# Seven-product down projection: the low part of the second weight sums is issued behind the additions of the second product group

## The chip, the cores and the metric

The kernel runs on one core of a Trainium2 chip. A core has TensorE (matrix products; PE in the profile, its weight loads PEld), VectorE (DVE), ScalarE (ACT), GpSimd (POOL) and SyncE (SP, which issues most transfers here). Each engine works through its own list of instructions in order, and the engines wait for one another by semaphores. The metric is the device time of one execution in microseconds (us), as the median of several runs.

## The reference

The reference is a decoder trunk of two layers on 512 tokens of width 1024. Each layer is a half-step SwiGLU feed-forward, a mixer (gated linear attention in layer 0, stick-breaking attention in layer 1) and a second half-step feed-forward, all in float32:

```python
def swiglu(h, w_gate, w_up, w_down):
    return (jax.nn.silu(h @ w_gate) * (h @ w_up)) @ w_down

for i in range(DEPTH):                       # DEPTH = 2, D_MODEL = 1024, D_FF = 2816, SEQ = 512
    x = x + 0.5 * swiglu(rmsnorm(x, ffn1_norm[i]), ffn1_w_gate[i], ffn1_w_up[i], ffn1_w_down[i])
    x = x + mixer(rmsnorm(x, mix_norm[i]))
    x = x + 0.5 * swiglu(rmsnorm(x, ffn2_norm[i]), ffn2_w_gate[i], ffn2_w_up[i], ffn2_w_down[i])
return rmsnorm(x, final_norm)
```

The change concerns the product with `w_down` in the four feed-forwards.

## The kernel before

**Numbers in two parts.** Each float32 operand is split into a high part (`wh`, `hh`, `nh`: a conversion on ScalarE, line 143 for weights, 852 for activations) and a low part (`wl`, `hl`, `nl`: the operand minus its high part, a subtraction on VectorE, lines 144 and 853). Each product is then three matmuls: high by high, low weight by high, high weight by low.

**Tiling.** The 512 tokens are the moving side and the rows of the weights are the contraction. The 2816 columns of the hidden layer are worked in six groups (`GROUPS`); the hidden columns of one group are multiplied by their rows of `w_down` and added to the residual tiles `xs` while the next groups' gate and up products run. For the groups 1 and 3 (`DOWN_SEVEN`), 512 hidden columns each, the down product is done by `seven_down`: the 2x2 blocks of weights and activations are combined so that seven block products do the work of eight. It is called twice for a group (`part` 0 and 1, each for 256 lower and 256 upper outputs), so four times in a feed-forward and sixteen times in the kernel.

**One call of `seven_down`** puts two entries on the feed, `body_1` and `body_2`. TensorE works in three PSUM tiles for each of two column blocks `m`: `w` (`ws`, lines 414 to 416), `z` (`zs`) and `q` (`qs`, both `m` in one bank). `prod` (line 396, its matmuls at line 401) issues six matmuls of 256 moving columns.

- `body_1`: a11 by b11 into `w`; ScalarE copies `w` to `z` (line 420); the first sums by t1 into `q` and two additions of `q` to x; then by t2 into `w`, each followed by an addition of `w` to x; then a2 by b21 into `z`, each followed by an addition of `z`.
- `body_2`: the second sums by t3 into `w`, copied to `u3` by ScalarE (line 448) and added to x; by b22 into `q`, added; a2 by t4 into `w`, added.

All additions go through `add` (line 405), whose instruction on VectorE stands at line 407. The sums of weight blocks are made on VectorE: the first at lines 385 and 386, the second at 392 and 393.

**How weights get split.** `Feed.start` (line 147) looks ahead: it splits the entries that come up, and for the entry after `body_1` of a seven it leaves the split out (the test of `e.second` and of `copied`). So the second sums of a call are split by `body_1` itself, at line 421: `v["second"].split(v["copied"])`. There the high part on ScalarE carries an order edge, `tc.issue_after(after)`, to the copy of `w` into `z`; the low part on VectorE has none. The second sums themselves, and the transfers behind them, were made at the start of `body_1`.

**What sets the order.** Nothing in this part of the kernel is pinned by hand. A planner orders each engine's instructions when the program is built: an instruction's place in the program is its priority, `ahead()` raises it, and of the instructions whose inputs are ready by the planner's own estimate of time the one with the highest priority goes first. `tc.issue_after(i)` adds, for what its block puts on the engine of `i`, the condition that it is placed behind `i`; it adds no semaphore. On the chip the order is then fixed, and an engine waits at an instruction whose semaphores have not come.

Of the kernel before, what the change touches and what calls it, by code (L numbers as in the profile page):

```python
# [10 lines left out]
F32 = mybir.dt.float32  # L11
# [4 lines left out]
ALU = mybir.AluOpType  # L16
# [14 lines left out]
def turns(t):  # L31

    return t.rearrange("p (two n) -> p n two", two=2)


def flat(ps):

    return ps.rearrange("p (n two) -> p two n", two=2)


def pair(t):

    return t.rearrange("p (two n) -> p two n", two=2)
# [3 lines left out]
def decoder(ctx: ExitStack, tc: tile.TileContext, a: dict, out: bass.AP):  # L47
    nc = tc.nc
# [12 lines left out]
    def psum(name, tag=None):  # L61
        if tag is None:
            tag = order[turn_[0] % 8]
            turn_[0] += 1
        return pp.tile([P, T], F32, tag=tag, bufs=banks[tag], name=name)
# [42 lines left out]
    class Entry:  # L108
# [11 lines left out]
                self.views = [view(ch.load()) for ch, view, _, _ in self.units]  # L120
            return self.views

        def split(self, after=None):
            if self.W is None:
                self.W = []
                for r, (_, _, n, m) in zip(self.view(), self.units):
                    self.W.append(self.parts(r, n, m, after))

        def parts(self, r, n, m, after):
            few = n * m < 1024  # L130
            if few:

                h, l = (
                    st["few"].tile([P, n * m], F32R, tag="v" + t, bufs=1, name="w" + t) for t in "hl"
                )
            else:
                h, l = (wp.tile([P, n * m], F32R, tag="w" + t, bufs=4, name="w" + t) for t in "hl")
            h, l = (t.rearrange("p (n m) -> p n m", m=m) for t in (h, l))
            pieces = r if isinstance(r, tuple) else (r,)
            for i, part in enumerate(pieces):  # L140
                k = slice(i * n // len(pieces), (i + 1) * n // len(pieces))
                with tc.issue_after(after) if after is not None else ExitStack():
                    nc.scalar.copy(h[:, k], part)  # L143
                nc.vector.tensor_tensor(out=l[:, k], in0=part, in1=h[:, k].bitcast(F32), op=ALU.subtract)  # L144
            return h, l

    class Feed:
# [51 lines left out]
    def ahead():  # L199

        return tc.high_priority(4000)
# [163 lines left out]
    def seven_down(pool, w, r0, hs, part):  # L365

        H = T // 2
        lower, upper = (  # L370
            Chunk(w[r0 : r0 + 4 * P, c : c + 256].rearrange("(f p) c -> p f c", p=P), 4, 256)
            for c in (part * 256, 512 + part * 256)
        )
        lower.few = upper.few = True
        v = {}

        def halves():

            lo, up = (c.load().rearrange("p (c two) d -> p two c d", two=2) for c in (lower, upper))
            return lo[:, 0], lo[:, 1], up[:, 0], up[:, 1]  # L380

        def sums_12(_):
            a11, _, a21, a22 = halves()
            s = v["s12"] = pool().tile([P, 4, 256], F32, tag="s", bufs=4, name="s12")
            nc.vector.tensor_tensor(out=s[:, 0:2], in0=a21, in1=a22, op=ALU.add)
            nc.vector.tensor_tensor(out=s[:, 2:4], in0=s[:, 0:2], in1=a11, op=ALU.subtract)
            return s

        def sums_34(_):
            a11, a12, a21, _ = halves()  # L390
            s = pool().tile([P, 4, 256], F32, tag="s", bufs=4, name="s34")
            nc.vector.tensor_tensor(out=s[:, 0:2], in0=a11, in1=a21, op=ALU.subtract)
            nc.vector.tensor_tensor(out=s[:, 2:4], in0=a12, in1=v["s12"][:, 2:4], op=ALU.subtract)
            return s

        def prod(ps, w, k0, m, b, first):
            for c in range(2):
                bh, bl = (turns(t) for t in hs[c][b])
                wh, wl = (t[:, k0 + c, m * P : (m + 1) * P] for t in w)
                for n, (l_, r_) in enumerate(((wh, bh), (wl, bh), (wh, bl))):  # L400
                    st["pe"] = nc.tensor.matmul(  # L401
                        ps, l_, r_, start=first and c + n == 0, stop=c == 1 and n == 2, skip_group_check=True
                    ).ins

        def add(m, up, col, ps):
            x = pair(xs[part * 2 + m + 4 * up][:, col * H : col * H + H])
            nc.vector.scalar_tensor_tensor(out=x, in0=ps, scalar=0.5, in1=x, op0=ALU.mult, op1=ALU.add)

        def body_1(W):
            a11, s, v["a2"] = W  # L410
            ws, zs, qs = [], [], []
            for m in range(2):
                ws.append(psum("ps_w")[:, 0:H])
                prod(ws[m], a11, 0, m, "b11", True)
            for m in range(2):


                zs.append(psum("ps_z")[:, 0:H])
                with ahead():
                    v["copied"] = nc.scalar.copy(zs[m], ws[m]).ins  # L420
            v["second"].split(v["copied"])
            yield

            ps = psum("ps_q")
            for m in range(2):
                qs.append(ps[:, m * H : (m + 1) * H])
                prod(qs[m], s, 0, m, "t1", m == 0)
            for m in range(2):
                add(m, 1, 1, flat(qs[m]))
            yield  # L430
            for m in range(2):
                prod(ws[m], s, 2, m, "t2", False)
                add(m, 0, 1, flat(ws[m]))
            yield
            for m in range(2):
                prod(zs[m], v["a2"], 0, m, "b21", False)
                add(m, 0, 0, flat(zs[m]))
            v["w"], v["q"] = ws, qs
            yield

        def body_2(W):
            (s,) = W
            ws, qs = v["w"], v["q"]

            u3 = pool().tile([P, 2, H], F32, tag="c", bufs=1, name="u3")
            for m in range(2):
                prod(ws[m], s, 0, m, "t3", False)
                nc.scalar.copy(pair(u3[:, m]), flat(ws[m]))
                add(m, 1, 1, pair(u3[:, m]))
            yield  # L450
            for m in range(2):
                prod(qs[m], s, 2, m, "b22", False)
            for m in range(2):
                add(m, 0, 1, flat(qs[m]))
            yield
            for m in range(2):
                prod(ws[m], v["a2"], 2, m, "t4", False)
                add(m, 1, 0, flat(ws[m]))
            yield

        units = [(lower, lambda t: halves()[0], 2, 256), (lower, sums_12, 4, 256), (lower, lambda t: halves()[1::2], 4, 256)]
        feed.q.append(Entry(units, body_1))
        feed.q.append(Entry([(lower, sums_34, 4, 256)], body_2))
        v["second"] = feed.q[-1]
        feed.q[-1].second, feed.q[-1].v = True, v
# [896 lines left out]
    class SB:  # L1362
# [28 lines left out]
        def evac_q(self, p, ps):  # L1391
            t = self.qp.tile([P, T], F32, tag="n", bufs=2, name="n")
            nc.vector.scalar_tensor_tensor(
                out=pair(t), in0=flat(ps), scalar=0.125, in1=pair(st["R"]), op0=ALU.mult, op1=ALU.mult
            )

            def parts(cast):
                for e in range(2):
                    own, oth = slice(e * 64, e * 64 + 64), slice(64 - e * 64, 128 - e * 64)
                    m = self.qp.tile([P, T], F32R, tag="mq", name="mq")  # L1400
                    cast(m[own], t[own])
                    nc.vector.tensor_tensor(out=m[oth], in0=t[own], in1=m[own].bitcast(F32), op=ALU.subtract)
                    self.qk[p, e, "q"] = m

            self.later.append(parts)
            if not self.hold:
                self.parts()
# [543 lines left out]
```

## Time and profile before

| | |
|---|---|
| median of 3 runs | 1775.71 us (1775.12 to 1776.97) |
| the profiled execution | 1776.0 us, span of its instructions 1774.1 us |
| granted TensorE clock in it | 0.999 |
| busy share of ScalarE, GpSimd | 61%, 3% |
| conversions to high parts of sums (line 143) | 176, 1053 ns each |
| additions of line 407 | 64 from `q`, 64 from `w`, 32 from `z`, 32 from `u3`; about 418 ns each |

The difference between the profiled execution and its span, 1.9 us, lies before the first and behind the last instruction. In the rows of a timeline the columns are the start and the duration in us, engine, line, operation, tile written and tiles read, shape and count; brackets hold the idle time of that engine just before and what is held to have ended it. Consecutive instructions of one kind are merged into a row with their count. "x<-ps_q,x x2" is thus a pair of additions. An instruction's end is where its row's start and duration add up; the next one may start a little before that.

### The profile page before, as it was taken

The numbers are of one execution on the slowest core, as the hardware profiler recorded it, in microseconds if no ns is written. First come the engines' busy times: TensorE is split into PE (matmuls) and PEld (weight loads), VectorE is DVE, ScalarE is ACT, GpSimd is POOL, SyncE is SP. The second block draws the span as 40 slices with busy tenths as digits, with TensorE's granted clock in tenths as the row PEclk, the third lists the DMA queues.
The fourth block names the chain that finished last, engine by engine and source line by source line (L and its number), as shares of the span: only waits on it lengthen the run. The fifth ranks groups of instructions, "written<-read, shape, count | busy, mean of one in ns | idle before, by whom it ended". The sixth has DMA issues, their size and how long they took to land.

```text
span 1774.1 us, 31336 instructions
## 1 busy us (share of the span) xinstructions
PE 1756.3 (99%) x12714; PEld 1631.8 (92%) x12714; DVE 1505.5 (85%) x2474; ACT 1074.7 (61%) x1883; POOL 55.6 (3%) x77
## 2 busy tenths in 40 slices
PE   9999999999999999999999999999999999999998
PEld 8999999889888899999889999999888888999997
DVE  8999797786888999888798988977898679998886
ACT  7556556554655565555656565655888745555555
POOL 0000000200000000000000000010000000000000
PEclk9999999999999999999999999999999999999999
DMA  5543434422122433334424344352212224424341
GB/s 167 155 122 105 137 105 146 113 72 73 49 95 96 126 113 120 119 120 125 134 92 131 102 125 133 100 132 83 84 49 73 71 95 131 130 97 127 112 127 71
DMA packets 186388, 193.14 MB, mean 109 GB/s; under 512 B 4930, under 2 KB 171124, under 8 KB 186244
## 3 DMA queue, kind: packets, MB, share of 16 engines
q1 hardware_dynamic: 177760, 175.91, 30.7%
q0 software_dynamic: 8240, 14.95, 4.7%
q8 instruction: 99, 1.62, 0.4%
q14 instruction: 45, 0.37, 0.1%
q10 hardware_dynamic: 244, 0.29, 0.0%
HBM read 175.17 MB, written 2.10 MB: 100 GB/s over the span
## 4 chain that ended last, share of the span: by engine, by line
PE 67%; DVE 21%; ACT 7%; issue 3%; DMA 1%; DVEq 0%; ACTq 0%; SPq 0%
PE ps_w L744 17%; PE ps_d L80 13%; PE ps_q L744 8%; PE ps_f L80 7%; DVE wl L144 6%; PE ps_t L80 4%; PE ps_z L744 4%; ACT wh L143 4%; PE ps_w L401 3%; PE ps_b L80 3%; PE ps_q L401 1%; DVE ts L862 1%; PE ps_z L1439 1%; DMA raw<-in_ffn_w_gate_dram 1%; DVE xn L846 1%
## 5 line engine op out<-in xcount | busy, mean ns | idle before, releaser
L144 DVE TENSOR_TENSOR wl<-raw,wh 128x1024 fp32r<-128x1024 f32 x241 | 255.7, 1062 | 47.6 <-ACT wh L143 47.0
L144 DVE TENSOR_TENSOR wl<-s,wh 128x1024 fp32r<-128x1024 f32 x176 | 215.2, 1223 | 82.6 <-ACT wh L143 80.2
L143 ACT CAST wh<-raw 128x1024 fp32r<-128x1024 f32 x241 | 221.9, 921 | 72.1 <-PE ps_f L80 22.6
L744 PE MATMUL ps_w<-th,wh 128*128 128x256 f32 x864 | 239.3, 277 | 0.4 <-ACT ps_z L772 0.2
L744 PE MATMUL ps_w<-th,wl 128*128 128x256 f32 x864 | 237.6, 275 | 0.0
L744 PE MATMUL ps_w<-tl,wh 128*128 128x256 f32 x864 | 237.6, 275 | 0.0
L143 ACT CAST wh<-s 128x1024 fp32r<-128x1024 f32 x176 | 185.3, 1053 | 35.4 <-DVE s L730 19.0
L744 PEld LDWEIGHTS ps_w<-th,wh 128*128 128x128 f32 x864 | 165.8, 192 | 1.8 <-ACT o L781 0.7
L80 PE MATMUL ps_f<-xh,wh 128*128 128x512 f32 x432 | 166.4, 386 | 0.0
L744 PEld LDWEIGHTS ps_w<-tl,wh 128*128 128x128 f32 x864 | 165.9, 192 | 0.0
L744 PEld LDWEIGHTS ps_w<-th,wl 128*128 128x128 f32 x864 | 165.8, 192 | 0.0
L80 PE MATMUL ps_f<-xh,wl 128*128 128x512 f32 x432 | 164.2, 380 | 0.5 <-DVE wl L144 0.5
L80 PE MATMUL ps_f<-xl,wh 128*128 128x512 f32 x432 | 163.9, 379 | 0.0
L80 PE MATMUL ps_d<-hl,wh 128*128 128x512 f32 x416 | 158.0, 380 | 1.7 <-DVE hl L853 1.7
L80 PE MATMUL ps_d<-hh,wh 128*128 128x512 f32 x416 | 158.0, 380 | 0.5 <-ACT hh L852 0.5
L80 PE MATMUL ps_d<-hh,wl 128*128 128x512 f32 x416 | 157.7, 379 | 0.0
L143 ACT CAST wh<-rawd 128x1024 fp32r<-128x1024 f32 (+1 forms) x100 | 83.1, 850 | 38.3 <-PE ps_d L80 24.9
L144 DVE TENSOR_TENSOR wl<-rawd,wh 128x1024 fp32r<-128x1024 f32 (+1 forms) x100 | 95.2, 965 | 10.2 <-ACT wh L143 10.2
L352 POOL DMA_DIRECT2D x<-d x53 | 45.9, 911 | 1565.5 <-ACT d L351 828.1
L80 PEld LDWEIGHTS ps_f<-xl,wh 128*128 128x128 f32 x432 | 81.6, 189 | 11.5
L80 PEld LDWEIGHTS ps_f<-xh,wl 128*128 128x128 f32 x432 | 81.7, 189 | 11.3 <-DVE wl L144 0.9
L80 PEld LDWEIGHTS ps_f<-xh,wh 128*128 128x128 f32 x432 | 81.7, 189 | 10.8
(355 smaller groups left out, 5334.4 us busy)
## 6 DMA issues: line engine op xcount, KB each, us to landing
raw<-in_ffn_w_gate_dram SPq DMA_DIRECT2D x43, 1024.0 KB, 5.3
raw<-in_ffn_w_up_dram SPq DMA_DIRECT2D x43, 1024.0 KB, 5.2
rawd<-in_ffn_w_down_dram SPq DMA_DIRECT2D x84, 512.0 KB, 3.6
x<-d POOLq DMA_DIRECT2D x53, 256.0 KB, 4.3
raw<-in_gla_w_in_dram SPq DMA_DIRECT2D x12, 1024.0 KB, 5.1
raw<-in_sb_w_in_dram SPq DMA_DIRECT2D x16, 512.0 KB, 3.6
raw<-in_gla_w_out_dram SPq DMA_DIRECT2D x4, 1024.0 KB, 4.9
raw<-in_sb_w_in_dram SPq DMA_DIRECT2D x4, 1024.0 KB, 5.1
```

The lines of the kernel that those rows point to most:

```text
L80: st["pe"] = nc.tensor.matmul(ps, l, r, start=first, stop=last).ins
L143: nc.scalar.copy(h[:, k], part)
L144: nc.vector.tensor_tensor(out=l[:, k], in0=part, in1=h[:, k].bitcast(F32), op=ALU.subtract)
L352: nc.gpsimd.dma_start(xs[k], d, accum_op=ALU.add)
L401: st["pe"] = nc.tensor.matmul(ps, l_, r_, start=first and c + n == 0, stop=c == 1 and n == 2, skip_group_check=True).ins
L744: st["pe"] = nc.tensor.matmul(o, l_, r_, start=first and j + n == 0, stop=j == 3 and n == 2, skip_group_check=True).ins
L846: nc.vector.scalar_tensor_tensor(out=t, in0=xs[k], scalar=g, in1=st["R"], op0=ALU.mult, op1=ALU.mult)
L862: nc.vector.tensor_tensor(out=o, in0=p, in1=q, op=ALU.subtract)
L1439: nc.tensor.matmul(o_, l_, r_, start=first, stop=last, skip_group_check=True)
```

## The change

`split` and `parts` get a second argument, `then`: an instruction behind which the low part's subtraction is placed on VectorE. `add` returns its instruction. `body_1` splits the second sums no longer ahead of the second product group but behind it and behind its two additions, and hands the second of these additions over as `then`. Conversion and subtraction of the second sums thus stand later in the program; the edge of the conversion to the copy is as before. Callers that pass no `then` are unchanged, among them the gate and up products, which split their own second sums at line 773.

```diff
-        def split(self, after=None):
+        def split(self, after=None, then=None):
             if self.W is None:
                 self.W = []
                 for r, (_, _, n, m) in zip(self.view(), self.units):
-                    self.W.append(self.parts(r, n, m, after))
-
-        def parts(self, r, n, m, after):
+                    self.W.append(self.parts(r, n, m, after, then))
+
+        def parts(self, r, n, m, after, then):
...
                 with tc.issue_after(after) if after is not None else ExitStack():
                     nc.scalar.copy(h[:, k], part)
-                nc.vector.tensor_tensor(out=l[:, k], in0=part, in1=h[:, k].bitcast(F32), op=ALU.subtract)
+                with tc.issue_after(then) if then is not None else ExitStack():
+                    nc.vector.tensor_tensor(out=l[:, k], in0=part, in1=h[:, k].bitcast(F32), op=ALU.subtract)
...
         def add(m, up, col, ps):
             x = pair(xs[part * 2 + m + 4 * up][:, col * H : col * H + H])
-            nc.vector.scalar_tensor_tensor(out=x, in0=ps, scalar=0.5, in1=x, op0=ALU.mult, op1=ALU.add)
+            return nc.vector.scalar_tensor_tensor(out=x, in0=ps, scalar=0.5, in1=x, op0=ALU.mult, op1=ALU.add).ins
...
                     v["copied"] = nc.scalar.copy(zs[m], ws[m]).ins
-            v["second"].split(v["copied"])
             yield
 
             ps = psum("ps_q")
...
             for m in range(2):
-                add(m, 1, 1, flat(qs[m]))
+                added = add(m, 1, 1, flat(qs[m]))
+            v["second"].split(v["copied"], added)
             yield
```

## The prediction

> **What bounds the kernel now.** I read the page first: busy shares, granted clock, the chain of work that ended last.
>
> ```profile
> span 1774.1 us, 31336 instructions
> ...
> PE 1756.3 (99%) x12714; PEld 1631.8 (92%) x12714; DVE 1505.5 (85%) x2474; ACT 1074.7 (61%) x1883; POOL 55.6 (3%) x77
> ...
> PEclk9999999999999999999999999999999999999999
> ...
> PE 67%; DVE 21%; ACT 7%; issue 3%; DMA 1%; DVEq 0%; ACTq 0%; SPq 0%
> ```
>
> TensorE is busy for 99% of the span at full clock, so time can come almost only from the few places where it stands still. The view of waits, cut to TensorE, names them; the view of line 401 (the matmuls of these down products) has the idle time of the weight loads.
>
> ```profile
> PE ps_w L401 <- ACT wh L143: 2.6, 9, 0.3
> ...
> PE ps_w L401 <- DVE x L407: 0.8, 3, 0.3
> ```
>
> ```profile
>   issue: 5.3, 12
> ```
>
> Nine and three make twelve waits of 0.28 us, in matmuls that write `w` in a down by seven products; the weight loads show the same twelve as 0.44 us each. There are sixteen calls, so twelve have the wait and four do not. Next I read the timelines of a call with it. First TensorE's matmuls and weight loads, then ScalarE, then VectorE:
>
> ```profile
> 134.31 0.28 PE L401 MATMUL ps_q<-hl,wh 128*128 128x256 f32 x1
> 134.43 0.28 PE L401 MATMUL ps_w<-hh,wh 128*128 128x256 f32 x1
> ...
> 135.65 0.28 PE L401 MATMUL ps_w<-hl,wh 128*128 128x256 f32 x1
> ...
> 136.99 0.28 PE L401 MATMUL ps_z<-hl,wh 128*128 128x256 f32 x1
> 137.56 0.35 PE L401 MATMUL ps_w<-nh,wh 128*128 128x256 f32 x1 [0.29 <-ACT wh L143]
> 137.74 0.28 PE L401 MATMUL ps_w<-nh,wl 128*128 128x256 f32 x1
> ```
>
> ```profile
> 137.53 0.19 PEld L401 LDWEIGHTS ps_w<-nh,wh 128*128 128x128 f32 x1 [0.45 <-issue]
> 137.64 0.19 PEld L401 LDWEIGHTS ps_w<-nh,wl 128*128 128x128 f32 x1
> ```
>
> ```profile
> 134.09 1.06 ACT L143 CAST wh<-s 128x1024 fp32r<-128x1024 f32 x1
> ...
> 136.52 1.04 ACT L143 CAST wh<-raw 128x1024 fp32r<-128x1024 f32 x1
> ```
>
> ```profile
> 133.75 0.69 DVE L730 TENSOR_TENSOR s<-s,raw 128x512 f32<-128x512 f32 x1
> 134.35 0.69 DVE L853 TENSOR_TENSOR hl<-o,hh 128x512 fp32r<-128x512 f32 x1
> 135.19 1.22 DVE L144 TENSOR_TENSOR wl<-s,wh 128x1024 fp32r<-128x1024 f32 x1 [0.15 <-ACT wh L143]
> 136.33 0.75 DVE L407 SCALAR_TENSOR_TENSOR x<-ps_q,x 128x256 f32<-128x256 f32 x2
> 137.00 0.75 DVE L407 SCALAR_TENSOR_TENSOR x<-ps_w,x 128x256 f32<-128x256 f32 x2
> 137.66 0.75 DVE L407 SCALAR_TENSOR_TENSOR x<-ps_z,x 128x256 f32<-128x256 f32 x2
> 138.32 0.68 DVE L144 TENSOR_TENSOR wl<-raw,wh 128x512 fp32r<-128x512 f32 x1
> ```
>
> The matmul at 137.56 is the first of the product with t3 and goes into `w`. It may not overwrite `w` before the first addition from `w` has read it: that one starts at 137.00, takes about 0.42 and ends at 137.41; the weight load follows at 137.53. The releaser printed, a conversion on ScalarE, is a coincidence: the one that ends at 136.52 + 1.04 = 137.56 ends after that load began, and the one it really needs, that of the second sums, ended at 134.09 + 1.06 = 135.15.
>
> Why is the addition from `w` so late? Its product ended at 135.27 (six matmuls 0.11 apart from 134.43, and the 0.28 of the last), 1.7 us before. VectorE is the late one: it has no idle time but 0.15, ahead of the low part of the second sums, which waits for its high part until 135.15. Behind it the additions from `q` stand ready: their product ended at 134.31 + 0.28 = 134.59.
>
> The steps between starts matter below: a subtraction of 512 elements is followed after 0.60 (133.75 to 134.35), a low part after 1.14 (135.19 to 136.33), a pair of additions after 0.67, one addition after 0.33.
>
> **The change part by part.** No instruction is added or removed and no transfer issued: the second sums and their loads were made at the start of the first entry. Sixteen conversions and sixteen low parts stand later in the program, behind twelve matmuls and two additions; each low part is held behind the additions from `q`. SP and POOL are not passed.
>
> *The conversion* keeps its edge to the copy, and between its old and new place the program holds nothing for ScalarE. It should run at the same time, at no cost; work that could pass it, the conversions of the next weights, comes later in the program still.
>
> *The low part* in the twelve calls. The new order on VectorE, by priority, is additions from `q`, low part, additions from `w`, from `z`. From the subtraction at 134.35: additions from `q` at 134.95 (ready since 134.59), low part at 135.62 (its high part is there since 135.15, so it no longer waits), additions from `w` at 135.62 + 1.14 = 136.76 instead of 137.00. The gain is the distance from where VectorE could have gone on to where it did, 135.19 - 134.95 = 0.24. In the last of the twelve:
>
> ```profile
> 1706.43 0.69 DVE L853 TENSOR_TENSOR hl<-o,hh 128x512 fp32r<-128x512 f32 x1
> 1707.24 1.22 DVE L144 TENSOR_TENSOR wl<-s,wh 128x1024 fp32r<-128x1024 f32 x1
> ```
>
> 1707.24 - 1706.43 - 0.60 = 0.21. I take the mean, 0.23. The low part itself ends later, at 135.62 + 1.22 = 136.84 against 136.41. TensorE wants it at the second weight load, now at 137.64 - 0.23 = 137.41, so 0.5 us is to spare; that wait of TensorE is the cover, and beyond it each us costs a us per call. Nobody else waits for the low part. Newly, the additions at the head of VectorE's queue wait for TensorE, with the low part behind them; here that wait is over.
>
> *What TensorE gets.* The first addition from `w` ends at 137.17, the weight load follows 0.12 later, the matmul at 137.33 instead of 137.56. Unhindered it would start 0.11 behind the matmul at 136.99, at 137.10. So some 0.2 of the stall stays, and after it the slow second step (137.56 to 137.74, 0.18 for 0.11). The whole stall costs 0.57 + 0.18 - 2 x 0.11 = 0.53, over twelve calls 6.3 us: the most there is to gain.
>
> The Trainium skill, Perfetto Trace Analysis (Tensor Engine Instruction), says that a matmul's end in the profile is computed from its size and not observed. By the idle times ahead of the matmuls the most would be 3.4 us, by their starts 6.3; the trace agrees with the page, since matmuls of 0.28 start 0.11 apart.
>
> *The four other calls*, the second of each feed-forward:
>
> ```profile
> 170.32 0.68 DVE L730 TENSOR_TENSOR s<-s,raw 128x512 f32<-128x512 f32 x1
> 172.81 1.22 DVE L144 TENSOR_TENSOR wl<-s,wh 128x1024 fp32r<-128x1024 f32 x1 [1.81 <-ACT wh L143]
> 173.96 0.75 DVE L407 SCALAR_TENSOR_TENSOR x<-ps_q,x 128x256 f32<-128x256 f32 x2
> 174.62 0.75 DVE L407 SCALAR_TENSOR_TENSOR x<-ps_w,x 128x256 f32<-128x256 f32 x2
> ```
>
> ```profile
> 172.49 0.28 PE L401 MATMUL ps_q<-hl,wh 128*128 128x256 f32 x1
> ...
> 175.28 0.28 PE L401 MATMUL ps_w<-nh,wh 128*128 128x256 f32 x1
> ```
>
> There VectorE is idle anyway, and the product into `q` ends at 172.77, as late as the high part. The additions from `q` take the low part's place at 172.81, the low part runs from 173.48 to 174.70, the additions from `w` stay at 174.62. TensorE does not wait at 175.28 and the low part has 0.5 us to spare. Cost: nothing.
>
> *The sum.* 12 x 0.23 = 2.7 us, against the profiled execution 1776.0 - 2.7 = 1773.3. The profiled execution lies 0.3 above the median of the runs, so the median should come to 1773.0. TensorE has no slack before the next waits that could swallow it, and VectorE and ScalarE move up by the same amount, as both are fed by this chain. For bounds: if only VectorE's idle time counts (0.15 at first, 1707.24 - 1706.43 - 0.69 = 0.12 at last) it is 12 x 0.14 = 1.7, so 1774.0; if the slow second step of 0.07 goes too, 12 x 0.30 = 3.6, so 1772.1. I take the middle, because it follows the starts, which are what rows of this very chain show.
>
> **The rivals.**
>
> *ScalarE releases TensorE* (the move does nothing). For: nine of twelve waits are put down to it. Against: the start of the weight load at 137.53, and three waits put down to the additions. Time 1775.7.
>
> *One addition from `w` goes ahead of the low part*, if the planner holds the high part for not yet there. Then that addition runs from 135.62 to 136.04, the low part from 135.95 to 137.17; TensorE's first weight load is free and its second, due at 137.18 (0.08 behind a matmul at 137.10, as 137.64 stands to 137.56), sees the low part 0.12 after its end, at 137.29. Some 0.1 of the 0.53 remains, the gain is 12 x 0.42 = 5 us: 1770.7. Against: the planner put the low part first before, so in its estimate the high part comes early.
>
> *Both additions from `w` go ahead.* The low part runs from 136.28 to 137.50, the second weight load at 137.62 is where it was: no gain in twelve calls. In the four others the twelve matmuls into `w` begin at 172.49 + 0.11 = 172.60, `w` is complete at 172.60 + 11 x 0.11 + 0.28 = 174.1, the low part ends at 174.13 + 0.33 + 1.22 = 175.68 and is seen at 175.80, where TensorE wants it at about 175.28: 0.5 each, 2 us: 1777.7.
>
> *Slower: the low part slips behind the additions from `z`.* It is now lower in the program and held back; if the planner's TensorE runs ahead of its ScalarE, all six additions go first. The last from `z` needs the matmul at 136.99, so starts at 137.30; the low part runs from 137.63 to 138.85, and the second weight load comes at 138.97 instead of 137.64: 1.33 by twelve, 16 us. In the four others `z` ends at 175.28 - 0.11 + 0.28 = 175.45, the low part at 177.0, 1.8 late, 7 us. Together 1798.7. It decides from 0.5 us on, the low part's margin; a single weight subtraction (0.60) that slips in already costs 0.1 per call. For: on the chip the high part came only at 135.15, when `q` was long complete. Against: then the planner would have sent the additions from `q` ahead already before; it sent the low part, and in the quoted timeline all of this part's VectorE work stands in program order.
>
> **How the numbers follow.** Forecast 56%; ScalarE 8%; one addition ahead 10%; both ahead 6%; slower 20%, anywhere from 1779 to 1799, as the slip may be partial. A difference of 0.2% (3.6 us) is about what a measurement of this kernel can tell from no change; the forecast of 2.7 lies inside it. I give a fifth of the forecast's chance, 12%, to a gain just over it (bound 3.6). Faster: 10 + 12 = 22%; within: 44 + 8 + 6 = 58%; slower: 20%. The forecast's own range is 1772 to 1774; the range for 8 in 10 leaves out most of the slower case and takes in one addition ahead, with the runs' own scatter of about 1 us: 1769.5 to 1780.
>
> **What would show it.** Right: in twelve calls VectorE's rows read subtraction, additions from `q`, low part with no idle time, additions from `w` 2.41 behind the subtraction's start (2.65 now), and TensorE's wait ahead of the product with t3 falls from 0.28 to 0.05, the twelve together to about 0.6 us. Wrong: the low part standing behind additions from `w` or `z`; a wait of TensorE for line 144 at the second weight load; the t3 matmul still at its old distance of 0.57 though VectorE's additions came earlier (ScalarE did release it); other waits of TensorE grown by what these twelve lost.

## The result and the profile after

| | before | changed |
|---|---|---|
| median of 22 runs each | 1775.55 us (1774.66 to 1778.32) | 1773.36 us (1771.74 to 1775.76) |
| span of the profiled execution | 1774.1 us | 1771.7 us |
| ratio of the runs | | 0.9986, 95% interval 0.998 to 0.9992 |

The change makes the kernel faster by 0.14%: 2.2 us by the medians, 2.5 by the ratio, with an interval of 1.4 to 3.6 us. Forecast were 2.7 us and 1773.0. From the page of the changed kernel, the lines that answer to those of before:

```profile
span 1771.7 us, 31344 instructions
...
PE 1756.1 (99%) x12714; PEld 1631.6 (92%) x12714; DVE 1504.2 (85%) x2474; ACT 1075.1 (61%) x1883; POOL 55.6 (3%) x77
...
PE 77%; DVE 15%; ACT 4%; issue 1%; DMA 1%; DVEq 0%; ACTq 0%; SPq 0%
```

The work is the same; the eight additional instructions on the page are semaphore instructions on VectorE. In the chain that ended last VectorE's share falls from 21% to 15%, and TensorE's grows by what VectorE, ScalarE and "issue" lose. Lines behind 143 have moved by one, so the matmuls of line 401 are now at 402 and the additions of 407 at 408. In the view of line 402 the weight loads' idle time ahead of the twelve matmuls has halved (5.3 before):

```profile
  issue: 2.5, 12
```

The first call, on VectorE and then on TensorE:

```profile
134.43 0.69 DVE L854 TENSOR_TENSOR hl<-o,hh 128x512 fp32r<-128x512 f32 x1
135.03 0.75 DVE L408 SCALAR_TENSOR_TENSOR x<-ps_q,x 128x256 f32<-128x256 f32 x2
135.70 1.22 DVE L145 TENSOR_TENSOR wl<-s,wh 128x1024 fp32r<-128x1024 f32 x1
136.83 0.75 DVE L408 SCALAR_TENSOR_TENSOR x<-ps_w,x 128x256 f32<-128x256 f32 x2
```

```profile
137.07 0.28 PE L402 MATMUL ps_z<-hl,wh 128*128 128x256 f32 x1
137.39 0.35 PE L402 MATMUL ps_w<-nh,wh 128*128 128x256 f32 x1
137.58 0.28 PE L402 MATMUL ps_w<-nh,wl 128*128 128x256 f32 x1
```

From the last matmul into `z` to the first by t3 (137.07 to 137.39) it is 0.32 where it was 0.57. VectorE has no idle time ahead of the low part, and the additions from `w` start 2.40 behind the subtraction at 134.43, as against 2.65. One of the four calls without a wait:

```profile
172.65 0.76 DVE L408 SCALAR_TENSOR_TENSOR x<-ps_q,x 128x256 f32<-128x256 f32 x2 [1.78 <-PE ps_q L402]
173.32 1.22 DVE L145 TENSOR_TENSOR wl<-s,wh 128x1024 fp32r<-128x1024 f32 x1
174.45 0.75 DVE L408 SCALAR_TENSOR_TENSOR x<-ps_w,x 128x256 f32<-128x256 f32 x2
```

There the idle time of VectorE now ends with the product into `q` and no longer with the high part, and nothing else moves.

### The profile page after: what moved, and what is told of

The parts are those of the page before. It is cut to its first block, busy times and chain, and to the rows that moved or that the text cites. A ratio compares the mean times of both kernels' runs of the same rounds, so it can differ in the third digit from the quotient of the medians.

```text
span 1771.7 us, 31344 instructions
## 1 busy us (share of the span) xinstructions
PE 1756.1 (99%) x12714; PEld 1631.6 (92%) x12714; DVE 1504.2 (85%) x2474; ACT 1075.1 (61%) x1883; POOL 55.6 (3%) x77
## 4 chain that ended last, share of the span: by engine, by line
PE 77%; DVE 15%; ACT 4%; issue 1%; DMA 1%; DVEq 0%; ACTq 0%; SPq 0%
PE ps_w L745 20%; PE ps_d L80 12%; PE ps_q L745 10%; PE ps_f L80 7%; PE ps_z L745 5%; PE ps_w L402 5%; PE ps_t L80 4%; DVE wl L145 3%; PE ps_b L80 3%; PE ps_q L402 2%; DVE ts L863 1%; PE ps_z L402 1%; PE ps_z L1440 1%; DVE xn L847 1%; DVE nl L854 1%
## 5 line engine op out<-in xcount | busy, mean ns | idle before, releaser
L80 PEld LDWEIGHTS ps_f<-xl,wh 128*128 128x128 f32 x432 | 81.6, 189 | 11.5
L80 PEld LDWEIGHTS ps_f<-xh,wh 128*128 128x128 f32 x432 | 81.7, 189 | 10.8
```

What stands on the lines that cost most here:

```text
L80: st["pe"] = nc.tensor.matmul(ps, l, r, start=first, stop=last).ins
```

## The experiments

Besides the medians, one number is taken from each trace: how late the matmuls of the seven products start, that is each distance from the start of the matmul before to that of one of theirs, where it is above 0.14 us, less the 0.11 us of an unhindered step, summed over the kernel. It comes from one execution of each kernel.

| | median, us | before beside it, us | ratio, 95% interval | matmuls late, us |
|---|---|---|---|---|
| before | 1775.55 | | | 6.2 |
| changed | 1773.36 | 1775.55 | 0.9986 (0.998 to 0.9992) | 3.4 |
| e1, moved only | 1776.46 | 1776.34 | 1.0 (0.9991 to 1.0009) | 6.2 |
| e2, behind one addition from `w` | 1771.45 | 1776.34 | 0.9972 (0.9962 to 0.9982) | 1.2 |
| e3, behind both from `w` | 1787.13 | 1776.34 | 1.0062 (1.0047 to 1.0077) | 18.3 |
| e4, behind all six | 1804.38 | 1776.34 | 1.0157 (1.0144 to 1.0171) | 36.2 |
| e5, changed, again | 1773.19 | 1776.04 | 0.9983 (0.9974 to 0.9992) | 3.4 |
| e6, `q` first | 1781.82 | 1776.04 | 1.0031 (1.002 to 1.0043) | 11.5 |
| e7, low part in two | 1770.22 | 1776.33 | 0.9968 (0.9955 to 0.998) | 0.0 |

Medians follow the last column: against before it goes by -2.8, 0, -5.0, +12.1, +30.0, -2.8, +5.3 and -6.2, the medians by -2.2, +0.1, -4.9, +10.8, +28.0, -2.9, +5.8 and -6.1. So what these kernels differ in is nearly all found at these matmuls.

**e1: the place in the program without the order edge.** Against the changed kernel:

```diff
-            v["second"].split(v["copied"], added)
+            v["second"].split(v["copied"])
```

> The split of the second sums stands at its new place in the program, but the low part is not held behind the additions from q. Theory (what counts is VectorE's order, and the order edge makes it): the planner still places the low part ahead of the additions from q, as in the kernel before, so the twelve waits of TensorE stay at 0.28 us each and the time is that of before, 1775.5 us. Rival (the later place in the program is enough): the order and the time of the changed kernel, 1773.4 us, with waits of 0.05 us.

Measured: the time of before. VectorE's rows, and TensorE's waits:

```profile
134.31 0.68 DVE L854 TENSOR_TENSOR hl<-o,hh 128x512 fp32r<-128x512 f32 x1
135.12 1.23 DVE L145 TENSOR_TENSOR wl<-s,wh 128x1024 fp32r<-128x1024 f32 x1
136.26 0.75 DVE L408 SCALAR_TENSOR_TENSOR x<-ps_q,x 128x256 f32<-128x256 f32 x2
```

```profile
PE ps_w L402 <- ACT wh L143: 3.1, 11, 0.3
```

The low part goes first although it now stands behind the additions in the program. All five engines' orders are those of the kernel before. That fits a planner that takes `q` to be ready later than the high part, the reverse of what the chip shows; its estimates were not looked into. The edge is what makes the change; e1 is a kernel of the order of before, and its time is the same to 0.1%.

**e2: behind the first addition from `w`.** Against the changed kernel:

```diff
-            v["second"].split(v["copied"], added)
...
-                add(m, 0, 1, flat(ws[m]))
+                added = add(m, 0, 1, flat(ws[m]))
+                if m == 0: v["second"].split(v["copied"], added)
```

> The low part of the second sums is held one addition further, behind the first addition from w. Theory (TensorE's matmul by t3 waits for the first addition from w, then the second weight load for the low part): the first addition from w ends 1.1 us earlier than in the changed kernel and no longer stops the first weight load; the second one sees the low part some 0.1 us late. Of the 0.285 us by which a call is still late in the changed kernel some 0.1 stays, so 12 x 0.18 = 2.2 us less: about 1771.2 us. Rival (a conversion on ScalarE releases TensorE): as the changed kernel, 1773.4 us.

Measured 1771.45 us, forecast 1771.2. VectorE, TensorE and ScalarE in the first call (this execution runs 1.6 us later in absolute terms):

```profile
136.58 0.75 DVE L408 SCALAR_TENSOR_TENSOR x<-ps_q,x 128x256 f32<-128x256 f32 x2
137.25 0.42 DVE L408 SCALAR_TENSOR_TENSOR x<-ps_w,x 128x256 f32<-128x256 f32 x1
137.58 1.22 DVE L145 TENSOR_TENSOR wl<-s,wh 128x1024 fp32r<-128x1024 f32 x1
```

```profile
138.62 0.28 PE L402 MATMUL ps_z<-hl,wh 128*128 128x256 f32 x1
138.73 0.28 PE L402 MATMUL ps_w<-nh,wh 128*128 128x256 f32 x1
138.85 0.38 PE L402 MATMUL ps_w<-nh,wl 128*128 128x256 f32 x1
139.06 0.28 PE L402 MATMUL ps_w<-nl,wh 128*128 128x256 f32 x1
```

```profile
138.15 1.04 ACT L143 CAST wh<-raw 128x1024 fp32r<-128x1024 f32 x1
```

The matmul by t3 follows after 0.11, without a wait, while the conversion at whose end it stood in the kernel before (136.52 to 137.56 there) runs on here until 139.19. ScalarE's order is unchanged, so that rival falls. The 0.1 us left per call has gone to the step from the second matmul to the third (0.21).

**e3: behind both additions from `w`.** Against the changed kernel:

```diff
-            v["second"].split(v["copied"], added)
...
-                add(m, 0, 1, flat(ws[m]))
+                added = add(m, 0, 1, flat(ws[m]))
+            v["second"].split(v["copied"], added)
```

> The low part of the second sums is held behind both additions from w, and the planner then also lets a low part of the next weights (512 elements, 0.60 us) in between the two. Theory (beyond 0.5 us of margin TensorE waits for the low part at its second weight load, us for us): the low part ends at 138.1 on the scale of the kernel before, 0.6 us later than the second weight load there can take in twelve calls, and 1.3 us in the four others: 7 + 5 = 12 us over the kernel before, about 1788 us, with waits of TensorE put down to the low part. Rival (VectorE's order behind the additions from q does not matter, since the wait is ScalarE's): 1773 to 1776 us.

Measured 1787.13 us, forecast 1788. VectorE and the waits of TensorE:

```profile
135.76 0.42 DVE L408 SCALAR_TENSOR_TENSOR x<-ps_w,x 128x256 f32<-128x256 f32 x1
136.09 0.69 DVE L145 TENSOR_TENSOR wl<-raw,wh 128x512 fp32r<-128x512 f32 x1
136.69 0.43 DVE L408 SCALAR_TENSOR_TENSOR x<-ps_w,x 128x256 f32<-128x256 f32 x1
137.03 1.22 DVE L145 TENSOR_TENSOR wl<-s,wh 128x1024 fp32r<-128x1024 f32 x1
```

```profile
PE ps_w L402 <- DVE wl L145: 11.3, 16, 0.8
```

All sixteen calls wait now, and for the low part. It ends at 138.25, and 0.60 of that is the foreign low part in between: holding an instruction back opens a place that the planner fills with something else.

The planner has also changed TensorE's order here, in all sixteen calls, and so it has in e4. The first matmul by t3 for the other column block needs the high part alone, and it now goes ahead of the matmul that needs the low part; in the first row below the two stand merged:

```profile
137.26 0.39 PE L402 MATMUL ps_w<-nh,wh 128*128 128x256 f32 x2
138.31 0.38 PE L402 MATMUL ps_w<-nh,wl 128*128 128x256 f32 x1 [0.66 <-DVE wl L145]
```

So the low part is wanted one matmul later than forecast, and a matmul ahead of it needs the second addition from `w`. That the forecast meets the sum is partly luck: by the starts, eight of the twelve calls lose 0.4 us against before (forecast 0.6), the last call of each feed-forward 1.1 (forecast 0.6), and the four others 1.1 (forecast 1.3).

**e4: behind the additions from `z`.** Against the changed kernel:

```diff
-            v["second"].split(v["copied"], added)
...
-                add(m, 0, 0, flat(zs[m]))
+                added = add(m, 0, 0, flat(zs[m]))
+            v["second"].split(v["copied"], added)
```

> The low part of the second sums is held behind all six additions of the first entry. Theory: the slower rival of the prediction made real, at its price: the second weight load 1.33 us late in twelve calls and 1.8 us in four, 23 us over the kernel before, about 1799 us; somewhat more where further low parts slip in. Rival (TensorE does not wait for the low part there): 1773 to 1776 us.

Measured 1804.38 us, 5 more than forecast. The waits are where they were expected:

```profile
PE ps_w L402 <- DVE wl L145: 22.7, 16, 1.4
```

What was not expected is in the last call of each feed-forward. TensorE there stands still twice in a row, and then runs at half speed. The first time it waits for the second addition from `w`, which stands behind a foreign low part that itself waits 0.61 us for its conversion. That low part on VectorE, the matmuls, and the windows' sums with the granted clock in the third column from the end:

```profile
284.60 0.69 DVE L145 TENSOR_TENSOR wl<-raw,wh 128x512 fp32r<-128x512 f32 x1 [0.61 <-ACT wh L143]
```

```profile
285.06 0.28 PE L402 MATMUL ps_w<-nh,wh 128*128 128x256 f32 x1
285.68 0.38 PE L402 MATMUL ps_w<-nh,wh 128*128 128x256 f32 x1 [0.34 <-DVE x L408]
287.47 0.38 PE L402 MATMUL ps_w<-nh,wl 128*128 128x256 f32 x1 [1.42 <-DVE wl L145]
```

```profile
284.00:288.00 4.00, 2.24 (x17) 1.86 (x17) 3.40 (x6) 1.51 (x3) 0.00 (x0) 0.99 0.00 0
288.00:291.00 3.00, 3.00 (x16) 3.00 (x16) 2.45 (x4) 0.74 (x2) 0.00 (x0) 0.50 0.38 122
```

From 287.9 to 291.3 the matmuls start 0.213 apart. Sixteen steps, each 0.1 longer, are 1.6 us in each of four calls, 6.5 us. Without them the matmuls are 23.5 us later than before, and 23 were forecast, so the half speed accounts for the miss. The Trainium skill, TensorE: Matmul & The Clock Gate (Part 1: The HAM clock gate), tells of a half-speed state after an idle window of about 3.4 us, left again after about 3.4 us of work. The trace agrees on the half speed and on its length of 3.4 us; but TensorE had stood still for only 2.4 us from start to start, with one matmul in the middle. In the four calls the half speed sets in 0.4 to 1.3 us after the second wait is over. In the other twelve calls a single distance of 1.7 us leaves the clock at 1.00, and so do the two of 0.6 and 1.1 us in the last calls of e3.

**e5: the changed kernel again.**

> The changed kernel once more, beside the kernel before on the same chip, to see how far its gain and the waits outside the twelve calls repeat. Theory: ratio to the kernel before 0.9986, twelve waits of 0.05 us before the matmul by t3. The waits of TensorE at the norms differ from one execution to the next by some tenths of a us, whatever the order. Rival (part of the gain is given back at the norms because of the new order): the waits at the norms at about 562 and 885 us are again 0.72 and 0.70 us, as in the first profile of the changed kernel, against 0.60 and 0.43 in that of the kernel before.

Measured: ratio 0.9983, twelve waits of 0.05 us. Waits of TensorE at the two norms, from the view of waits cut to 550 to 900 us, first of the kernel before, then e1 (same order), changed, e5 (same order as changed):

```profile
PE ps_R L80 <- ACT sh L579: 1.0, 2, 0.6
```

```profile
PE ps_R L80 <- ACT sh L580: 1.1, 2, 0.6
```

```profile
PE ps_R L80 <- ACT sh L580: 1.4, 2, 0.7
```

```profile
PE ps_R L80 <- ACT sh L580: 1.2, 2, 0.8
```

The single waits trade places: the one at 885 us, 0.70 in the first profile of the changed kernel, is 0.42 in e5 as before the change. The sums differ by 0.1 to 0.2 us between executions of one order and by 0.1 to 0.4 between the orders. Whether some 0.2 us of the 2.8 is given back there stays open. TensorE's whole idle time outside the seven products is 6.7 and 7.0 us in the two executions of the order of before, and 7.4 and 6.6 in the two of the changed one, so nothing more shows.

**e6: the product into `q` first.** The kernel before, in whose `body_2` the product by t3 (with its copies and additions) and that by b22 (with its additions) change places; the low part stands where it stood:

```diff
-            for m in range(2):
-                prod(ws[m], s, 0, m, "t3", False)
-                nc.scalar.copy(pair(u3[:, m]), flat(ws[m]))
-                add(m, 1, 1, pair(u3[:, m]))
-            yield
             for m in range(2):
                 prod(qs[m], s, 2, m, "b22", False)
             for m in range(2):
                 add(m, 0, 1, flat(qs[m]))
             yield
+            for m in range(2):
+                prod(ws[m], s, 0, m, "t3", False)
+                nc.scalar.copy(pair(u3[:, m]), flat(ws[m]))
+                add(m, 1, 1, pair(u3[:, m]))
+            yield
```

> The kernel before, with one thing changed: the second entry makes its product into q first and that by t3 into w second, so the order of the additions to x differs. Theory (TensorE waits until w, which it wants to overwrite, has been read): the first product of the entry now overwrites q, whose additions end at 137.08 on the scale of the kernel before, where TensorE comes at 137.10; at most 0.1 of the 0.53 us per call stays, 5 us less in twelve calls. But the product by the last sums into w now follows directly on that by t3, and has to wait for ScalarE's copy of w into u3: some 0.2 us in each of sixteen calls, 3 us more. Together about 2 us under the kernel before, 1773.5 us, with waits put down to the copy in line 448. Rival (the first product of the second entry waits for a conversion on ScalarE): the twelve waits of 0.28 us stay where they are and the new ones are added: about 1779 us.

Measured 1781.82 us, 8 more than forecast, and on the wrong side of before; it lies nearer to the rival's 1779, so the trace has to decide. The additions from `q` and the first matmuls of the second entry in the first call:

```profile
136.00 0.75 DVE L407 SCALAR_TENSOR_TENSOR x<-ps_q,x 128x256 f32<-128x256 f32 x2
```

```profile
136.69 0.28 PE L401 MATMUL ps_z<-hl,wh 128*128 128x256 f32 x1
136.90 0.35 PE L401 MATMUL ps_q<-hh,wh 128*128 128x256 f32 x1
137.08 0.28 PE L401 MATMUL ps_q<-hh,wl 128*128 128x256 f32 x1
```

The half that separates the theories holds: the twelve waits of 0.28 us are gone. The first matmul of the entry, now into `q`, starts 0.21 to 0.23 behind the last into `z`, once the additions from `q` have ended (136.75); with the slow second step 0.18 of the 0.53 us per call stays, where at most 0.1 was forecast. TensorE waits until VectorE has read the bank that its next product goes into. The cost of the copies was put too low, at 3 us where the starts give 9.3. ScalarE and TensorE in a call of the other kind:

```profile
176.98 0.38 ACT L453 COPY u<-ps_w 128x256 f32<-128x256 f32 x1 [2.29 <-PE ps_w L401]
177.66 1.06 ACT L143 CAST wh<-raw 128x1024 fp32r<-128x1024 f32 x1 [0.30 <-PE ps_w L401]
178.62 0.37 ACT L453 COPY u<-ps_w 128x256 f32<-128x256 f32 x1
```

```profile
178.07 0.28 PE L401 MATMUL ps_w<-t,wh 128*128 128x256 f32 x1
179.04 0.38 PE L401 MATMUL ps_w<-nh,wh 128*128 128x256 f32 x1 [0.69 <-ACT u L453]
```

In eight calls the planner has put a conversion of the next weights between the two copies, and TensorE waits for it too: 0.97 from start to start. In the order of before the product into `q` covers both copies.

**e7: the low part in two.** `body_1` has the half for t3 made behind the additions from `q`, and the other half behind the first addition from `w`:

```diff
...
+                    low(slice(0, n // 2), part[:, 0 : n // 2], then)
+                    self.rest = lambda i: low(slice(n // 2, n), part[:, n // 2 : n], i)
...
-                add(m, 0, 1, flat(ws[m]))
+                added = add(m, 0, 1, flat(ws[m]))
+                if m == 0:
+                    v["second"].rest(added)
```

> The changed kernel with the low part of the second sums made by two subtractions of 512 elements: the half that the product by t3 needs behind the additions from q, the other behind the first addition from w. Theory (TensorE at the first two weight loads of the second entry waits for the first addition from w and for the first half of the low part, and for nothing else): on the scale of the kernel before the first half ends at 136.30, the first addition from w at 136.63, both ahead of TensorE at 137.10, so none of the 0.53 us per call is left. Against the kernel before 12 x 0.53 = 6.3 us less, 1.2 us less than with the low part in one piece behind the first addition: ratio about 0.9965. Rival (the remaining 0.1 us per call with the one piece is a cost of TensorE's own after a change of product, not a wait for the low part): the third matmul by t3 still starts 0.21 instead of 0.11 behind the second, and the ratio stays at 0.9972.

Measured 1770.22 us, ratio 0.9968. TensorE in the first call:

```profile
137.00 0.28 PE L409 MATMUL ps_z<-hl,wh 128*128 128x256 f32 x1
137.11 0.28 PE L409 MATMUL ps_w<-nh,wh 128*128 128x256 f32 x1
137.23 0.28 PE L409 MATMUL ps_w<-nh,wl 128*128 128x256 f32 x1
137.34 0.28 PE L409 MATMUL ps_w<-nl,wh 128*128 128x256 f32 x1
```

No distance between starts is left above 0.14 in any of the sixteen calls. The 0.1 us of e2 was a wait for the low part. The median is 1.2 us below e2's, as forecast; the intervals of the two overlap, so this last step is shown by the trace and not by the times. e2 and e7 are the fastest versions: every run of theirs, up to 1772.85 and 1770.94 us, lies below the changed kernel's median. The ratios of e2 and of the changed kernel to before still touch (0.9982 and 0.998), so here too the starts are the better evidence.

## Why the prediction was right

*What bounds the kernel.* Right: TensorE's twelve waits held 6.2 us (6.3 worked out), and taking all of them away brought 6.1 us in e7.

*Who releases TensorE.* Right: the addition from `w`. The profile's releaser, ScalarE's conversion, was a coincidence: both the next conversions on ScalarE and the low part with the additions on VectorE start when the conversion of the second sums is done, about 135.1, and their work happens to take equally long. e2 takes the wait away with ScalarE's order unchanged, and e6 leaves 0.1 us of it with the conversions ahead of it in the same place. One word is wrong: the matmuls by t3 do not overwrite `w`, they add to it (`prod` is called with `first` False); they must wait for the reading addition all the same.

*The order.* Right in all sixteen calls, for the edge. The reason given, that VectorE's work goes by priority in program order, does not hold by itself: in e1 the low part comes later in the program and is still put first. In four later gate and up products additions moved by a place or two as well, on VectorE alone, and no wait of TensorE came of them.

*The size.* Right: 0.23 per call was worked out from the starts. In the first call the distance went from 0.57 to 0.32, in the last from 0.54 to 0.32, and the trace's lateness fell by 2.8 us in all. The bound by VectorE's idle time alone (1.7) was too low, the one with the slow second step (3.6) too high: that step is 0.18 as before. Medians say 2.2 and 2.9 in two sets of runs. That they come so near to 2.7 is in part luck, since the 22 runs of the changed kernel alone spread over 4 us; the starts are what bears the size out. The prediction held a change under 0.2% for hardly to be told from none; the interval of the ratio does leave out 1.

*The four other calls and the low part's margin.* Right: no cost there. In the first call of the changed kernel the low part ends at 136.92 and the weight load that reads it starts at 137.47, so the margin is 0.55; in e3 and e4, where the low part ends some 1.3 and 2.0 us later, every call waits for it.

*The rivals.* One addition ahead was priced at 1770.7, e2 gave 1771.45. Both ahead was priced at 1777.7 and gave 1787.13, because the low part of other weights (0.60 in every call) slipped in, which the price left out, and TensorE's order changed. The slower rival was priced at 1798.7 and gave 1804.38, because of TensorE's clock. All three orders had to be forced by an edge; the planner does not make them from this change.

## What to carry to other kernels

When an engine is full and its consumer waits, look for the order of its work that serves the consumer's next need first: here 2.8 of 6.2 us came from sending two short, ready additions ahead of a subtraction whose input was not there, and the rest from letting a third one pass and cutting the subtraction in two. Where a wait is put down to an engine, compare the start of the waiting weight load with the end of the named instruction, and measure what a wait costs from start to start, not by the idle time shown. An instruction's place in the program may count for nothing: in e1 it changed no engine's order. An order edge does count, but whatever it holds back has a margin, here 0.5 us, and the planner may rearrange the rest: in e3 and e4 other work slipped into the place and TensorE's order changed too.

## What the runs showed of the hardware

TensorE ran at half its clock for 3.4 us after standing still in two steps of 0.6 and 1.8 us, from start to start, with one matmul between them (e4, 285.06 to 287.47 us, granted clock 0.50 from 288 to 291, and three more places like it), and did not after a single one of 1.7 us. The matmul after one that waited starts 0.18 to 0.21 us behind it instead of 0.11 (0.18 in before and changed, 0.21 in e3, e4 and behind the copies of e6), so a wait costs 0.07 to 0.1 us more than its own length. Two profiles of one order (before and e1) differ by 1.2 us in span, half of the effect studied here: the single waits have to be compared, not the spans.
